# Sample attention over the paged cache: from split 128-column products to plain fp32 products of 32 columns

## The chip, the cores and the metric

The kernel runs on one core of one Trainium2 chip. The metric is the time of one execution on the device in microseconds (us). The engines of a core run side by side: TensorE (PE in the profile: matrix products; its loads of the stationary operand are PEld), VectorE (DVE), ScalarE (ACT), GpSimd (POOL), and SyncE (SP), which issues most of the transfers between DRAM and the on-chip memory SBUF. TensorE writes its products to PSUM. A matrix product holds one operand still (the stationary one: at most 128 rows, the length that is summed, by 128 columns) and streams the other past it (the moving one: up to 512 columns).

## What is computed

One layer of a decoder for 1024 prompt tokens and 64 sample tokens (8 sequences of 8 new tokens): a SwiGLU feed-forward half, a mixing stage (8 heads of forgetting attention and 4 heads of gated linear attention), and a second feed-forward half, all in fp32. The part that matters here is the attention of the sample tokens over a paged cache. Each sequence has 2048 cached positions in 16 pages of 128, found through a page table, for 8 heads of 64:

```python
def fox_sample(q, k, v, logf, pool_k, pool_v, pool_logf, page_table):
    DB, S, H, D = q.shape
    P = page_table.shape[1] * PAGE_SIZE
    pk = pool_k[page_table].reshape(DB, P, H, D)
    pv = pool_v[page_table].reshape(DB, P, H, D)
    ...
    s_past = (jnp.einsum('bqhd,bkhd->bhqk', q, pk).astype(jnp.float32) * scale
              + cn[..., :, None] + jnp.swapaxes(after, 1, 2)[:, :, None, :])
    s_new = (jnp.einsum('bqhd,bkhd->bhqk', q, k).astype(jnp.float32) * scale
             + cn[..., :, None] - cn[..., None, :])
    causal = jnp.tril(jnp.ones((S, S), dtype=bool))
    s_new = jnp.where(causal, s_new, -jnp.inf)
    p = jax.nn.softmax(jnp.concatenate([s_past, s_new], axis=-1), axis=-1).astype(v.dtype)
    return (jnp.einsum('bhqk,bkhd->bqhd', p[..., :P], pv)
            + jnp.einsum('bhqk,bkhd->bqhd', p[..., P:], v))
```

`after` is the sum of the log-forgets of the cached positions behind a key; `cn` the running sum over the new tokens.

## The kernel before

Products of full precision are built from a reduced form of fp32 (float32r), which TensorE takes in one pass: an operand is split into a rounded part `hi` and the rest `lo` (line 143: ScalarE copies with rounding, VectorE subtracts), and a product is the sum of hi·hi, hi·lo and lo·hi. A product of plain fp32 operands is given to TensorE as it is, and the trace records it as two passes, each with its own weight load (line 1228 has 224 such products of 64 columns in its full tiles and 448 records).

The dense products of the feed-forward halves and projections (line 210, line 440) make up most of the work. The program emits them in a fixed order, and `tick` (line 155) hands out other work between them: after so many microseconds of dense products it lets the attention emit a piece. For the sample attention the rate is 1.1 pieces a microsecond (line 985). So it lies spread between dense products, from about 1305 to 1680 us of the span. The order on each engine's queue is that in which the program is laid out, where readiness lets a later product go before an earlier one.

`sample` (line 759) handles two sequences (a pair, `p`) at a time, in steps:

- `fetch` (line 781) loads two pages (128 x 2 x 512 numbers, 512 KB) into a buffer `pr`, five of which exist, three steps ahead of use. Key pages come by SP's queue (`page`, line 749) with the page number read into a register; value pages, and every second key page of the first pair, by an indirect transfer that GpSimd issues (line 791). Every fourth page brings with it the biases `af` (16 rows: hi and lo for 8 heads).
- `cut` (line 798) splits the buffer into `ph` and `pl`, one step ahead, two buffers each.
- `key_step` (line 841): the stationary operand is `qz`, 128 columns: 64 for the hi part of a sequence's queries and 64 for the lo part, with the heads laid out so that pair `a` of heads has 16 columns of each half and zeros elsewhere. For each of four pairs of heads there are two products (lines 854 and 855, with `ph` and `pl`) of 256 moving columns; a ninth product (line 856) adds the biases through `sel`, 16 rows by 128 columns. Each second step, `total` (line 830) adds the halves and keeps the greatest score.
- `new_keys` (line 861): the scores of the new tokens, eight products of 64 columns and one of 16 rows, twice a pair. `soft` (line 870): exponential and scaling of all 2112 scores of 128 rows. `queries` (line 819) places the next pair's queries in the two `qz` tiles, the same two for every pair.
- `turn` (line 877): transposes of the weights, split into `pT`.
- `value_step` (line 894): for each of two pages two products (lines 902 and 903) of 512 moving columns, stationary the 64 hi and 64 lo columns of all heads of one sequence; all heads meet all heads, and only the matching blocks are used. After the eighth step, two products for the new tokens' values (line 906, 64 rows), and the sum goes to `ob`. `out` (line 910) adds the halves and takes the matching blocks, by four products with `fold` (line 914).

For a pair there are 16 key steps, 5 turns and 16 value steps; the next pair's key steps alternate with the value steps.

Of the kernel before, what the change touches and what calls it, by code (L numbers as in the profile page):

```python
# [55 lines left out]
def together(*gens):  # L56
    """Pieces of several streams in turn"""
    live = list(gens)
    while live:
        for g in list(live):  # L60
            if next(g, live) is live:
                live.remove(g)
            else:
                yield


class Feed:
    """Weights in the order of their use: loaded two ahead, split one ahead"""
# [49 lines left out]
class Step:  # L118
# [24 lines left out]
    def split(self, hi, lo, src):  # L143
        """src = hi + lo, hi rounded"""
        self.nc.scalar.copy(hi, src)  # L145
        self.nc.vector.tensor_tensor(out=lo, in0=src, in1=hi.bitcast(F32), op=ALU.subtract)  # L146
# [28 lines left out]
    def beside(self, g, quick=False, begin=False):  # L175
        """Adds a stream of norm or evacuation pieces; begin: its first piece now"""
# [20 lines left out]
    def gemm(self, w, c0, n, packed=False):  # L197
        """Full-precision product of split operands. packed: hi has lo's columns behind its own 64, the sum of the halves is left to do."""
# [15 lines left out]
    def square(self, yk, k, n, pool, sums):  # L214
        """Adds a row of squares to one of two partial sums."""
# [12 lines left out]
    def ptile(self, kind):  # L228
        """A bank of PSUM for the norms: col, col2 or rows"""
# [3 lines left out]
    def rms(self, sums, n, pool, kind):  # L233
        """1/rms of every token, windows of tokens on the partitions"""
# [7 lines left out]
    def rms_quick(self, y, n, pool):  # L242
        """1/rms of the first n tokens, by as many engines as can help"""
# [20 lines left out]
    def rms_col(self, col, m, pool):  # L264
        """1/rms from m pairs of columns of sums"""
# [7 lines left out]
    def stat(self, sums, n, pool, out):  # L273
        """Piece that finishes the sums of a chunk"""
# [9 lines left out]
    def rms_rows(self, dg, n):  # L284
        """[P, n] with 1/rms of every token on all partitions"""
# [5 lines left out]
    def need(self, key):  # L291
        """Emits what is left of the norms up to key"""
# [3 lines left out]
    def norm(self, y, y0, c0, n, pool, post=None, pre=None, v=None, key=None):  # L296
        """post: y = res + rmsnorm(y) * gain, also to DRAM; pre: U = split(rmsnorm(y) * gain). v: list that takes 1/rms. Yields between pieces."""
# [57 lines left out]
    def ffn(self, w_gu, w_dn, f):  # L355
        """Jobs for y = (silu(U wg) * (U wu)) wd, transposed, for the columns of f. f.first(i): before chunk i is used first;
        f.after(c0, n, sums): what follows a finished chunk of y."""
# [9 lines left out]
        def gated(t, src, x):  # L367
            """t = silu(src), or twice that where f.tanh; x: src on the partitions of t"""
# [175 lines left out]
NRAW = 5  # L544
NAF = 3
NHL = 2
AHEAD = 3
# [7 lines left out]
class StepA(Step):  # L555
# [169 lines left out]
    def past_bias(self, pool):  # L725
        """Sum of the log-forgets after every cached position, split, to DRAM."""
# [22 lines left out]
    def page(self, g, dst, pool):  # L749
        """Loads page g of the table from the pool."""  # L750
# [8 lines left out]
    def sample(self, X, ps):  # L759
        """Paged forgetting attention of the sample group, two sequences at a time; yields between pieces."""  # L760
# [3 lines left out]
        tmp = lambda nm, shape, dt: X.tile(shape, dt, name=nm, tag="ob", bufs=1)  # L764
# [7 lines left out]
        qsmp = cst("qsmp", [P, 2, 4, TS], F32R)  # L772
        ksmp = cst("ksmp", [P, 2, 4, TS], F32R)
        vsmp = cst("vsmp", [TS, 2, 512], F32R)
        for s in range(2):
            nc.sync.dma_start(qsmp[:, s].bitcast(F32), self.qs[s, :, :, TP:].rearrange("a p t -> p a t"))
        self.page_dmas = []
        pages = []
        raws, parts, afs = {}, {}, {}

        def fetch(n):
# [4 lines left out]
            for i in range(2):  # L786
                g = 2 * p * NPG + 2 * t + i
# [5 lines left out]
            if kind == "K" and t % 2 == 0:  # L793
                afs[p, t // 2] = af = X.tile([16, 512], F32R, name=self.uid("af"), tag="af", bufs=NAF)
                o = t % 8 // 2 * 512
                nc.sync.dma_start(af.bitcast(F32), self.afs[2 * p + t // 8].rearrange("s h g t -> (s h) (g t)")[:, o:o + 512])

        def cut(n):
            if n in parts or n >= len(pages):
                return  # L800
            hi = X.tile([P, 2, 512], F32R, name=self.uid("ph"), tag="hi", bufs=NHL)
            lo = X.tile([P, 2, 512], F32R, name=self.uid("pl"), tag="lo", bufs=NHL)
            self.split(hi, lo, raws[n])
            parts[n] = hi, lo
# [8 lines left out]
        qz = []  # L813
        for i in range(2):
            z = cst(f"qz{i}", [P, 4, P], F32R)
            nc.scalar.copy(z, self.zero[:, :1].unsqueeze(2).to_broadcast([P, 4, P]))
            qz.append(z)

        def queries(p):
            for b in (2 * p, 2 * p + 1):  # L820
                for s in range(2):
                    for e in range(2):
                        r = slice(64 * e, 64 * e + 64)
                        o = qz[b % 2][r].rearrange("p a n -> p (a n)")
                        o = bass.AP(tensor=o.tensor, offset=o.offset + 64 * s + 8 * e, ap=[o.ap[0], [P + 16, 4], [1, 8]])
                        (nc.gpsimd if p else nc.vector).tensor_copy(o, qsmp[r, s, :, 8 * b:8 * b + 8].bitcast(F32))
# [3 lines left out]
        def total(p, e2, sp, n, o, add, w):  # L830
            """Sum of the two parts of scores, with the greatest"""
            R = slice(64 * e2, 64 * e2 + 64)
            sl = X.tile([64, 512], F32, name=self.uid("sl"), tag="sl", bufs=1)
            if add is None:
                nc.scalar.copy(sl[:, :n], sp[64:, :n])
            else:
                nc.vector.tensor_tensor(out=sl[:, :n], in0=sp[64:, :n], in1=add, op=ALU.add)
            nc.vector.tensor_tensor_reduce(out=S[p][R, o:o + n], in0=sp[:64, :n], in1=sl[:, :n], scale=1.0, scalar=-3.0e38,
                                           op0=ALU.add, op1=ALU.max, accum_out=mx[p][R, w:w + 1])

        def key_step(n, p, t):
            kh, kl = page_step(n)
            q = qz[t // 8]
# [3 lines left out]
            j = t % 2  # L847
            if j == 0:
                box["sp"] = ps.tile([P, 512], F32, name=self.uid("sp"), tag="S", bufs=2)
            sp = box["sp"]  # L850
            cs = slice(256 * j, 256 * j + 256)
            so = sp[:, cs].rearrange("p (g t) -> p g t", t=P)
            for a in range(4):
                nc.tensor.matmul(so, q[:, a, :], kh[:, :, a * P:(a + 1) * P], start=(a == 0), stop=False)  # L854
                nc.tensor.matmul(so, q[:, a, :], kl[:, :, a * P:(a + 1) * P], start=False, stop=False)  # L855
            nc.tensor.matmul(sp[:, cs], sel, afs[p, t // 2][:, cs], start=False, stop=True)  # L856
            if j:
                g = t % 8 // 2
                total(p, t // 8, sp, 512, 512 * g, None, g)

        def new_keys(p):
            for e2 in range(2):
                sp = ps.tile([P, 512], F32, name=self.uid("sp"), tag="S", bufs=2)
                for a in range(4):
                    for s in range(2):
                        nc.tensor.matmul(sp[:, :TS], qz[e2][:, a, :], ksmp[:, s, a, :], start=(a == 0 and s == 0), stop=False)
                nc.tensor.matmul(sp[:, :TS], sel, cnr, start=False, stop=True)
                total(p, e2, sp, TS, NK, smask[:, 2 * p + e2, :], 4)

        def soft(p):  # L870
# [4 lines left out]
            nc.scalar.activation(out=s, in_=s, func=AF.Copy, scale=m[:, 7:8])  # L875

        def turn(p, j):
            if j == 0:
                box["pT"] = X.tile([P, NPG, 2, P], F32R, name=self.uid("pT"), tag="pT", bufs=1)
                box["pN"] = X.tile([64, 2, P], F32R, name=self.uid("pN"), tag="pN", bufs=1)  # L880
            pT, pN, s = box["pT"], box["pN"], S[p]
            tp = ps.tile([P, 512], F32, name=self.uid("tp"), tag="pt", bufs=1)
            if j < 4:
                for i in range(4):
                    nc.tensor.transpose(tp[:, P * i:P * i + P], s[:, (4 * j + i) * P:(4 * j + i + 1) * P], self.ident)
                src = tp.rearrange("p (g e c) -> p g e c", e=2, c=64)
                h, l = pT[:, 4 * j:4 * j + 4, :, :64], pT[:, 4 * j:4 * j + 4, :, 64:]
            else:
                nc.tensor.transpose(tp[:64, :P], s[:, NK:], self.ident)
                src = tp[:64, :P].rearrange("p (e c) -> p e c", c=64)  # L890
                h, l = pN[:, :, :64], pN[:, :, 64:]
            self.split(h, l, src)
# [768 lines left out]
```

## Time and profile before

| | |
|---|---|
| median of 3 runs | 2524.99 us |
| lowest and highest | 2522.19 and 2528.23 us |
| span of the profiled execution | 2529.9 us |
| mean clock granted to TensorE in it | 0.984 of full |
| HBM read, written | 284.39 MB, 43.69 MB |

The span is that of another execution than the three timed ones, from its first instruction to its last; it has no other time of its own. In the profile a line such as "L854 PE MATMUL sp<-ph,qz 128*128 128x256 f32 x256 | 67.9, 291 | 2.4 <-ACT ph L145 2.4" means: line 854 of the kernel, TensorE, products into `sp` from `ph` and `qz`, stationary 128 rows by 128 columns, moving 128 rows by 256 columns, 256 of them; 67.9 us busy together, 291 ns each in the mean; TensorE idle for 2.4 us just before them, all of it until ScalarE had done `ph` on line 145. A line of the timeline gives the start (us from the span's start), the time to the end of the group, and the group. A line of the windows view gives the stretch, its length, the busy time and number of instructions of PE, PEld, DVE, ACT and POOL, the granted clock, the mean busy share of the 16 DMA engines and GB/s. In the view of one line's instructions, three durations are least, median and greatest in ns, then the first and last start. In the view of waits: who waited for whom, us in total, times, longest. Products on TensorE overlap their neighbours, so that what one costs is read from the distance between starts rather than from its own duration.

### The profile page before, as it was taken

What the parts mean: (1) busy time and instruction counts of PE and PEld (TensorE: products, weight loads), DVE (VectorE), ACT (ScalarE), POOL (GpSimd) and SP (SyncE); (2) the same over time, 40 slices, a digit from 0 to 9 for tenths busy, and PEclk for the clock granted to TensorE, in tenths of its full rate; (3) what the DMA queues carried; (4) which work ended last, traced back from release to release, by engine and by line L of the source; (5) the groups of instructions that cost most, each with busy time, mean ns of one, the idle gap of its engine ahead of it and who ended that gap; (6) DMA issues with size and microseconds to landing.
All of it is one profiled execution on the core that took longest, in us unless ns stands there. A gap on an engine that the chain in (4) does not pass through costs nothing.

```text
span 2529.9 us, 40161 instructions
## 1 busy us (share of the span) xinstructions
PE 2469.8 (98%) x15524; PEld 2221.8 (88%) x15524; DVE 1343.8 (53%) x2500; ACT 1021.2 (40%) x1752; POOL 404.8 (16%) x426
## 2 busy tenths in 40 slices
PE   7999999999999999999999999999999999999997
PEld 7799999999899788999897787878788989999997
DVE  7223232322358746655567777757776675333345
ACT  5311112111134556553547666646455544222222
POOL 3000000000013210100233644540010131000001
PEclk9999999999999999999999999999899999999998
DMA  3111111111134776643457776765554544222222
GB/s 121 65 42 44 49 42 43 50 42 43 68 123 131 229 225 190 186 148 102 154 183 239 249 252 223 225 188 155 148 167 136 191 129 149 83 82 83 84 76 88
DMA packets 177024, 330.71 MB, mean 131 GB/s; under 512 B 25265, under 2 KB 100482, under 8 KB 176834
## 3 DMA queue, kind: packets, MB, share of 16 engines
q1 hardware_dynamic: 165170, 289.87, 36.2%
q0 software_dynamic: 11664, 38.28, 4.8%
q8 instruction: 122, 2.00, 0.3%
q14 instruction: 68, 0.56, 0.1%
HBM read 284.39 MB, written 43.69 MB: 130 GB/s over the span
## 4 chain that ended last, share of the span: by engine, by line
PE 39%; issue 4%; DMA 3%; DVE 3%; POOL 2%; ACT 2%; POOLq 0%; ACTq 0%; DVEq 0%; SPq 0%
PE mm L210 17%; PE mm L440 10%; PE pa L1228 1%; DMA pr<-in_cv,rows 1%; PE sp L854 1%; DMA wr<-in_wout 1%; POOL pr L791 1%; PE sp L855 1%; PE tp L1084 1%; DVE wl L146 1%; PE po L1099 1%; PE po L903 1%; PE po L902 1%; ACT wh L145 1%; PE sp L856 1%
## 5 line engine op out<-in xcount | busy, mean ns | idle before, releaser
L210 PE MATMUL mm<-ub,wh 128*128 128x320 f32 (+2 forms) x3776 | 771.5, 299 | 0.1
L210 PE MATMUL mm<-ua,wh 128*128 128x512 f32 (+2 forms) x2288 | 639.1, 364 | 3.8 <-ACT ua L351 1.7
L210 PEld LDWEIGHTS mm<-ub,wh 128*128 128x128 f32 (+1 forms) x3776 | 608.3, 189 | 9.9 <-issue 3.1
L146 DVE TENSOR_TENSOR wl<-wr,wh 128x1024 fp32r<-128x1024 f32 (+1 forms) x294 | 356.8, 1214 | 407.6 <-ACT wh L145 404.7
L145 ACT CAST wh<-wr 128x1024 fp32r<-128x1024 f32 (+1 forms) x294 | 301.4, 1025 | 647.5 <-PE mm L210 305.0
L210 PE MATMUL mm<-ub,wl 128*128 128x320 f32 (+1 forms) x1872 | 553.2, 296 | 0.3 <-DVE wl L146 0.3
L210 PEld LDWEIGHTS mm<-ua,wh 128*128 128x128 f32 (+1 forms) x2288 | 400.8, 191 | 64.9 <-issue 4.9
L210 PE MATMUL mm<-ua,wl 128*128 128x512 f32 (+1 forms) x1136 | 408.4, 360 | 0.8 <-DVE wl L146 0.7
L210 PEld LDWEIGHTS mm<-ub,wl 128*128 128x128 f32 x1872 | 354.4, 189 | 0.5 <-DVE wl L146 0.5
L440 PE MATMUL mm<-hl,wh 128*128 128x256 f32 (+4 forms) x1088 | 354.1, 326 | 0.0
L440 PE MATMUL mm<-hh,wh 128*128 128x256 f32 (+2 forms) x1040 | 339.9, 327 | 0.8 <-DVE y L450 0.8
L440 PE MATMUL mm<-hh,wl 128*128 128x256 f32 (+2 forms) x1040 | 333.0, 321 | 0.0
L210 PEld LDWEIGHTS mm<-ua,wl 128*128 128x128 f32 x1136 | 217.0, 191 | 33.2 <-DVE wl L146 1.8
L450 DVE TENSOR_TENSOR y<-y,mm 128x256 f32<-128x256 f32 (+2 forms) x272 | 130.0, 503 | 185.6 <-PE mm L440 184.9
L224 POOL TENSOR_TENSOR ss<-ss,sq 128x256 f32<-128x256 f32 (+1 forms) x46 | 44.0, 959 | 1146.6 <-ACT sq L220 1145.1
L440 PEld LDWEIGHTS mm<-hl,wh 128*128 128x128 f32 (+1 forms) x1088 | 206.1, 189 | 19.6 <-issue 8.6
L440 PEld LDWEIGHTS mm<-hh,wh 128*128 128x128 f32 x1040 | 196.7, 189 | 18.7 <-issue 4.2
L440 PEld LDWEIGHTS mm<-hh,wl 128*128 128x128 f32 x1040 | 196.9, 189 | 12.3 <-issue 0.6
L146 DVE TENSOR_TENSOR pl<-pr,ph 128x1024 fp32r<-128x1024 f32 x128 | 155.9, 1224 | 69.9 <-ACT ph L145 68.9
L791 POOL DMA_INDIRECT pr<-in_cv,rows x128 | 164.2, 1283 | 117.5 <-DVE pl L146 64.3
L145 ACT CAST ph<-pr 128x1024 fp32r<-128x1024 f32 x128 | 133.6, 1048 | 98.8 <-PE sp L854 45.7
L379 DVE TENSOR_TENSOR sg<-mm,sg 128x256 f32<-128x256 f32 (+4 forms) x112 | 55.8, 498 | 185.9 <-PE mm L210 184.3
(244 smaller groups left out, 2799.8 us busy)
## 6 DMA issues: line engine op xcount, KB each, us to landing
wr<-in_wgu SPq DMA_DIRECT2D x137, 512.0 KB
wr<-in_wd SPq DMA_DIRECT2D x60, 512.0 KB
pr<-in_ck SPq DMA_DIRECT2D x112, 256.0 KB
wr<-in_win SPq DMA_DIRECT2D x50, 512.0 KB
wr<-in_wout SPq DMA_DIRECT2D x32, 512.0 KB
h<-y SPq DMA_DIRECT2D x12, 512.0 KB
x<-h SPq DMA_DIRECT2D x24, 256.0 KB
wr<-in_wd SPq DMA_DIRECT2D x20, 256.0 KB
```

The source lines that it names most:

```text
L145: self.nc.scalar.copy(hi, src)
L146: self.nc.vector.tensor_tensor(out=lo, in0=src, in1=hi.bitcast(F32), op=ALU.subtract)
L210: nc.tensor.matmul(out, a, x[:, k, o:o + n], start=(k == 0 and j == 0), stop=(k == KB - 1 and j == len(ops) - 1))
L224: (nc.gpsimd if odd else nc.vector).tensor_tensor(out=s, in0=s, in1=sq[:, :n], op=ALU.add)
L379: nc.vector.tensor_tensor(out=out, in0=u, in1=t, op=ALU.mult)
L440: nc.tensor.matmul(pds[e], a, b, start=(i == 0 and j == 0), stop=(i == len(g) - 1 and j == len(ops) - 1))
L450: nc.vector.tensor_tensor(out=yk, in0=yk, in1=pds[e], op=ALU.add)
L791: nc.gpsimd.indirect_dma_start(out=raw[:, i], out_offset=None, in_=A["ck" if kind == "K" else "cv"].rearrange("g p n -> (g p) n"), in_offs ...
L854: nc.tensor.matmul(so, q[:, a, :], kh[:, :, a * P:(a + 1) * P], start=(a == 0), stop=False)
L855: nc.tensor.matmul(so, q[:, a, :], kl[:, :, a * P:(a + 1) * P], start=False, stop=False)
L856: nc.tensor.matmul(sp[:, cs], sel, afs[p, t // 2][:, cs], start=False, stop=True)
L902: nc.tensor.matmul(po, pT[:, g, e2, :], vh[:, i], start=(g == 0), stop=False)
```

## The change

The sample attention takes plain fp32 operands: pages are used as they land, without `cut`. The queries and new keys and values, which lie in DRAM as two parts, are loaded and added up once. A stationary operand has 32 columns, those of one pair of heads for both sequences of the pair (2 sequences x 2 heads x 8 queries), and its output goes to one of four groups of 32 PSUM partitions: pair of heads `a` at 32a. A key step's buffer holds two pages of one sequence, with zeros in the other sequence's 16 columns; a value step's holds one page of each sequence. The bias product comes first, once for 512 columns, with `sel` and the biases padded with zeros to 128 rows. There are eight page buffers instead of five, loaded six steps ahead instead of three; each pair of sequences has its own of two `qz` tiles; the softmax's scaling moves to the copy of the output. One accumulation and one `out` serve both sequences. The constants `sel` and `smask` follow the new layout, and `fold` goes. The diff also drops the docstrings, which is left out here.

```diff
-NRAW = 5
+NRAW = 8
 NAF = 3
-NHL = 2
-AHEAD = 3
+AHEAD = 6
...
+        q2 = X.tile([P, 2, 4, TS], F32, name="q2", tag="two", bufs=2)
...
+        nc.vector.tensor_tensor(out=qf, in0=q2[:, 0], in1=q2[:, 1], op=ALU.add)
...
+        afz = [cst(f"afz{i}", [P, 512], F32R) for i in range(NAF)]
+        qz = [cst(f"qz{i}", [P, 4, 2, 32]) for i in range(2)]
+        for z in qz:
+            nc.gpsimd.memset(z, 0.0)
...
-                g = 2 * p * NPG + 2 * t + i
+                if kind == "K":
+                    g = (2 * p + t % 2) * NPG + 4 * (t // 4) + 2 * (t % 4 // 2) + i
+                else:
+                    g = (2 * p + i) * NPG + t
...
-            for m in range(n, n + NHL):
-                cut(m)
-            return parts[n]
+            return raws[n]
...
+        def total(p, sp, n, o, add, w):
+            nc.vector.tensor_tensor_reduce(out=S[p][:, o:o + n], in0=sp[:, :n], in1=add, scale=1.0, scalar=-3.0e38,
+                                           op0=ALU.add, op1=ALU.max, accum_out=mx[p][:, w:w + 1])
...
         def key_step(n, p, t):
-            kh, kl = page_step(n)
-            q = qz[t // 8]
+            raw = page_step(n)
+            j, hf, s = t // 4, t % 4 // 2, t % 2
...
+            if t % 4 == 0:
                 box["sp"] = ps.tile([P, 512], F32, name=self.uid("sp"), tag="S", bufs=2)
+                nc.tensor.matmul(box["sp"], sel, afs[p, j], start=True, stop=False)
             sp = box["sp"]
             for a in range(4):
-                nc.tensor.matmul(so, q[:, a, :], kh[:, :, a * P:(a + 1) * P], start=(a == 0), stop=False)
-                nc.tensor.matmul(so, q[:, a, :], kl[:, :, a * P:(a + 1) * P], start=False, stop=False)
-            nc.tensor.matmul(sp[:, cs], sel, afs[p, t // 2][:, cs], start=False, stop=True)
+                nc.tensor.matmul(sp[32 * a:32 * a + 32, 256 * hf:256 * hf + 256], qz[p % 2][:, a, s, :], raw[:, :, a * P:(a + 1) * P], start=False, stop=(t % 4 == 3))
+            if t % 4 == 3:
+                total(p, sp, 512, 512 * j, self.zero[:, :1].to_broadcast([P, 512]), j)
...
         def new_keys(p):
+            sp = ps.tile([P, 512], F32, name=self.uid("sp"), tag="S", bufs=2)
+            nc.tensor.matmul(sp[:, :TS], sel, cnr, start=True, stop=False)
+            for s in range(2):
                 for a in range(4):
+                    nc.tensor.matmul(sp[32 * a:32 * a + 32, :TS], qz[p % 2][:, a, s, :], kf[:, a, :], start=False, stop=(s == 1))
+            total(p, sp, TS, NK, smask[:, p, :], 4)
...
-            nc.scalar.activation(out=s, in_=s, func=AF.Copy, scale=m[:, 7:8])
...
+                nc.scalar.copy(pT[:, 4 * j:4 * j + 4, :].rearrange("p g c -> p (g c)"), tp)
...
         def value_step(n, p, t):
-            vh, vl = page_step(n)
+            raw = page_step(n)
...
-                nc.tensor.matmul(po, pT[:, g, e2, :], vh[:, i], start=(g == 0), stop=False)
-                nc.tensor.matmul(po, pT[:, g, e2, :], vl[:, i], start=False, stop=False)
...
+            for a in range(4):
+                r = slice(32 * a, 32 * a + 32)
+                nc.tensor.matmul(po[r], pT[:, t, r], raw[:, :, a * P:(a + 1) * P], start=(t == 0), stop=False)
+            if t == NPG - 1:
+                for a in range(4):
+                    r = slice(32 * a, 32 * a + 32)
+                    nc.tensor.matmul(po[r], pN[:, r], vf[:, :, a * P:(a + 1) * P], start=False, stop=True)
+                box["ob"] = X.tile([P, 2 * P], F32, name=self.uid("ob"), tag="ob", bufs=2)
+                nc.scalar.activation(out=box["ob"], in_=po, func=AF.Copy, scale=mx[p][:, 7:8])
...
-                nc.tensor.matmul(ot[:, 64 * a:64 * a + 64], ob[:, a * P:(a + 1) * P], fold, start=True, stop=True)
+            for s in range(2):
+                nc.tensor.transpose(ot[:, s * P:(s + 1) * P], ob[:, s * P:(s + 1) * P], self.ident)
```

More of the change, by code (lines that the diff above doesn't have):

```diff
@@ L792, in fetch @@
                                                  in_offset=bass.IndirectOffsetOnAxis(ap=rows[:, g:g + 1], axis=0))
[L793 to L804, printed above, removed]
+            if kind == "K" and t % 4 == 0:
+                j = t // 4
+                afs[p, j] = af = afz[(4 * p + j) % NAF]
+                for s in range(2):
+                    nc.sync.dma_start(af[16 * s:16 * s + 16].bitcast(F32), self.afs[2 * p + s].rearrange("s h g t -> (s h) (g t)")[:, 512 * j:512 * j + 512])
         def page_step(n):
@@ L904, in value_step @@
-            if j == 7:
-                for s in range(2):
-                    nc.tensor.matmul(po, box["pN"][:, e2, :], vsmp[:, s, :], start=False, stop=(s == 1))
-                box["ob"] = X.tile([P, 512], F32, name=self.uid("ob"), tag="ob", bufs=1)
-                nc.scalar.copy(box["ob"], po)
-        def out(b):
+            po, pT = box["po"][:, :2 * P], box["pT"]
+            for a in range(4):
+                r = slice(32 * a, 32 * a + 32)
+                nc.tensor.matmul(po[r], pT[:, t, r], raw[:, :, a * P:(a + 1) * P], start=(t == 0), stop=False)
@@ L945, in sample @@
                     paged("K", p + 1, ks.pop(0))
-            outs = {}
-            for t in range(16):
+            for t in range(NPG):
                 paged("V", p, t)
-                if t % 8 == 7:
-                    outs[t // 8] = len(steps)
-                if t == 9 or t == 15:
-                    if t == 15 and not ks:
-                        steps.append(lambda: None)
-                    steps.append(lambda b=2 * p + t // 10: out(b))
                 if ks:
@@ L958, in sample @@
                         scored(p + 1)
+            steps.append(lambda: None)
+            steps.append(lambda p=p: out(p))
+        for z in afz:
+            nc.scalar.copy(z, self.zero[:, :1].to_broadcast([P, 512]))
         for n in range(AHEAD):
@@ L961, in sample @@
         queries(0)
+        k2 = X.tile([P, 2, 4, TS], F32, name="k2", tag="two", bufs=2)
         for s in range(2):
-            nc.sync.dma_start(ksmp[:, s].bitcast(F32), self.ks[s, :, :, TP:].rearrange("a p t -> p a t"))
-            nc.sync.dma_start(vsmp[:, s].rearrange("t (a v) -> t a v", v=P).bitcast(F32), self.vss[:, s].rearrange("a t v -> t a v"))
-        fold = cst("fold", [P, 64])
-        smask = cst("smask", [64, NB, TS])
-        nc.sync.dma_start(fold, A["fold"])
+            nc.sync.dma_start(k2[:, s], self.ks[s, :, :, TP:].rearrange("a p t -> p a t"))
+        kf = cst("kf", [P, 4, TS])
+        nc.vector.tensor_tensor(out=kf, in0=k2[:, 0], in1=k2[:, 1], op=ALU.add)
+        v2 = X.tile([TS, 2, 512], F32, name="v2", tag="v2", bufs=1)
+        for s in range(2):
+            nc.sync.dma_start(v2[:, s].rearrange("t (a v) -> t a v", v=P), self.vss[:, s].rearrange("a t v -> t a v"))
+        vf = cst("vf", [P, 2, 512])
+        nc.gpsimd.memset(vf, 0.0)
+        for i in range(2):
+            nc.vector.tensor_tensor(out=vf[:TS, i], in0=v2[:, 0], in1=v2[:, 1], op=ALU.add)
+        pN = cst("pN", [P, P])
+        nc.gpsimd.memset(pN, 0.0)
+        smask = cst("smask", [P, NB // 2, TS])
         nc.sync.dma_start(smask, A["smask"])
-        selr = tmp("selr", [16, P], F32)
+        selr = tmp("selr", [P, P], F32)
         nc.sync.dma_start(selr, A["sel"])
-        sel = cst("sel", [16, P], F32R)
+        sel = cst("sel", [P, P], F32R)
         nc.scalar.copy(sel, selr)
-        cnr = cst("cnr", [16, TS], F32R)
-        nc.sync.dma_start(cnr.bitcast(F32), self.cns.rearrange("s h t -> (s h) t"))
+        cnr = cst("cnr", [P, TS], F32R)
+        nc.scalar.copy(cnr, self.zero[:, :1].to_broadcast([P, TS]))
+        for s in range(2):
+            nc.sync.dma_start(cnr[16 * s:16 * s + 16].bitcast(F32), self.cns.rearrange("s h t -> (s h) t"))
         for _ in range(LEAD):
@@ L1597, in consts @@
     c['later']=((i[:,None]//16==i[None]//16)&(i[:,None]%16>i[None]%16)).astype(np.float32)
[L1598 to L1600 removed]
+    t=np.arange(64); s_,q_=i[:,None,None]//16%2,i[:,None,None]%8; p_=np.arange(4)[None,:,None]
+    c['smask']=np.where((t//8==2*p_+s_)&(t%8<=q_),0,-1e30).astype(np.float32)
     r=np.ones((128,512+64),np.float32); r[:,0:512:128]=0; r[:,512::8]=0; c['rst']=r
[L1602 to L1604 removed]
+    s=np.zeros((128,128),np.float32)
+    for a in range(32):
+        h=a%8
+        o=32*(h//2)+16*(a//16)+8*(h%2)
+        s[a,o:o+8]=1
     c['sel']=s
```

82 lines of the change are left out of this document (19 added, 63 removed).

## The prediction

> **What bounds the kernel now.** I read the page's busy table first, then the windows view for the stretch in which the sample attention runs (its pages are loaded from 1305 us on, its last product starts at 1679 us), then that stretch by line and shape.
>
> ```profile
> PE 2469.8 (98%) x15524; PEld 2221.8 (88%) x15524; DVE 1343.8 (53%) x2500; ACT 1021.2 (40%) x1752; POOL 404.8 (16%) x426
> ...
> 1300.00:1680.00 380.00, 368.85 (x1875) 296.99 (x1876) 270.80 (x373) 234.48 (x289) 198.00 (x174) 0.98 0.71 228
> ```
>
> TensorE is busy 98% of the span, and in this stretch 368.85 of 380 us; VectorE 271, ScalarE 234, the DMA share 0.71. So TensorE's own time counts one for one, and work taken off ScalarE and VectorE counts only through TensorE's 11 idle us. By line and shape:
>
> ```profile
> L146 DVE TENSOR_TENSOR pl<-pr,ph 128x1024 fp32r<-128x1024 f32 x128 | 155.9, 1224 | 69.9 <-ACT ph L145 68.9
> L145 ACT CAST ph<-pr 128x1024 fp32r<-128x1024 f32 x128 | 133.6, 1048 | 98.8 <-PE sp L854 45.7 <-PE po L902 24.6 <-DMA pr<-in_cv,rows 18.4
> L854 PE MATMUL sp<-ph,qz 128*128 128x256 f32 x256 | 67.9, 291 | 2.4 <-ACT ph L145 2.4
> L855 PE MATMUL sp<-pl,qz 128*128 128x256 f32 x256 | 64.4, 284 | 0.9 <-DVE pl L146 0.9
> L902 PE MATMUL po<-ph,pT 128*128 128x512 f32 x128 | 52.6, 411 | 6.8 <-ACT ob L908 5.0 <-ACT ph L145 1.7
> L903 PE MATMUL po<-pl,pT 128*128 128x512 f32 x128 | 52.4, 410 | 1.1 <-DVE pl L146 0.9
> L856 PE MATMUL sp<-af,sel 16*128 16x256 f32 x64 | 24.0, 377 | 0.0
> ```
>
> The splits of the pages (289 us of two engines) go away whole, but TensorE waited only 2.4 + 0.9 + 6.8 + 1.1 = 11.2 us in front of these products. The question is what the products themselves cost. A row's mean overlaps its neighbours, so I price by the distance between starts in the timeline of TensorE:
>
> ```profile
> 1403.84 0.28 PE L855 MATMUL sp<-pl,qz 128*128 128x256 f32 x1
> 1403.95 0.28 PE L854 MATMUL sp<-ph,qz 128*128 128x256 f32 x1
> 1404.08 0.28 PE L855 MATMUL sp<-pl,qz 128*128 128x256 f32 x1
> 1404.28 0.38 PE L856 MATMUL sp<-af,sel 16*128 16x256 f32 x1
> 1404.59 0.50 PE L902 MATMUL po<-ph,pT 128*128 128x512 f32 x1
> 1404.93 0.62 PE L210 MATMUL mm<-ua,wh 128*128 128x512 f32 x2
> 1405.39 0.39 PE L903 MATMUL po<-pl,pT 128*128 128x512 f32 x1
> 1405.62 0.40 PE L902 MATMUL po<-ph,pT 128*128 128x512 f32 x1
> ```
>
> A 256-column product takes 0.12 us, a 512-column one 0.23. The 16-row bias product costs more than itself: 0.20 to it instead of 0.12, 0.31 over it, 0.34 over the next instead of 0.23: 0.08 + 0.31 + 0.11 = **0.50 us**, of which 0.11 is its own stream. So an excursion from the full array to a tile of it and back costs **0.39 us**.
>
> **The change part by part.** *Price of a plain fp32 product.* Line 1297 (one such product, 512 columns) is recorded as two passes:
>
> ```profile
> 1923.87 1.02 PE L1297 MATMUL rb<-gsq,ones 128*128 128x512 f32 x2
> 1924.33 1.02 PE L210 MATMUL mm<-ua,wh 128*128 128x512 f32 x2
> 1925.18 0.40 PE L210 MATMUL mm<-ua,wl 128*128 128x512 f32 x1
> ```
>
> From 1923.87 to 1925.18 are 1.31 us; two dense products take 0.46 of it, so two passes of 512 columns take 0.85, and one pass of 256 columns 0.21. Each page step of the new kernel has four products of two passes: 8 x 0.21.
>
> *What four column positions make of it.* No row shows two tiles of the array at work, so I bound it. One after another: 8 x 0.2135 = 1.71 us. All four side by side: 2 x 0.2135 = 0.43. I take the middle that the timeline's strict order suggests: its rows start one by one as the program has them. The second pass of a position needs the columns that the first one occupies, and waits; the next position's first pass stands behind it and can run beside it. So one pass-time goes by per position, and one at the end: 5 x 0.2135 = **1.07 us**.
>
> *Excursions.* Every page step now leaves the full array. 0.39 us is for weights of 128 columns; a load of few columns is shorter:
>
> ```profile
> L706 PEld LDWEIGHTS lt<-ident,st x9: 80/85/88, 875.4 to 1059.0; 128*8 128x8 f32 x8, 64*8 64x8 f32 x1
> L856 PEld LDWEIGHTS sp<-af,sel x64: 180/181/185, 1324.3 to 1613.9; 16*128 16x128 f32 x64
> ```
>
> 0.085 against 0.181 for 8 and 128 columns, so 32 columns save 0.08 once: **0.31 us**. The bounds are 0 (column positions might need no change-over) and 0.39. Here a page speaks against the change: the Trainium skill, TensorEngine Tiling (Array Packing), section Key Properties, says that changing the tiling mode drains the engine, while changing the tile does not. The row tiles above agree (0.39 us); no run yet shows column tiles; by the page the 128 excursions stay in the sum, without it they leave it.
>
> *Sum of TensorE's sample work, before.* Besides the page steps:
>
> ```profile
> 1364.48 0.97 PE L866 MATMUL sp<-ksmp,qz 128*128 128x64 f32 x8
> 1365.39 0.29 PE L867 MATMUL sp<-cnr,sel 16*128 16x64 f32 x1
> 1365.61 0.73 PE L210 MATMUL mm<-ua,wh 128*128 128x512 f32 x2
> 1366.17 0.28 PE L854 MATMUL sp<-ph,qz 128*128 128x256 f32 x1
> ...
> 1676.73 0.40 PE L903 MATMUL po<-pl,pT 128*128 128x512 f32 x1
> 1677.06 0.73 PE L906 MATMUL po<-vsmp,pN 64*128 64x512 f32 x2
> 1677.72 0.50 PE L210 MATMUL mm<-ua,wh 128*128 128x512 f32 x1
> 1678.06 0.40 PE L210 MATMUL mm<-ua,wl 128*128 128x512 f32 x1
> ...
> 1678.98 1.00 PE L914 MATMUL ot<-fold,ob 128*128 128x64 f32 x8
> 1679.79 0.71 PE L210 MATMUL mm<-ua,wh 128*128 128x512 f32 x2
> 1680.34 0.39 PE L210 MATMUL mm<-ua,wl 128*128 128x512 f32 x1
> ```
>
> Each group is the distance to its follower plus what the follower is late. Keys 64 x 8 x 0.1175 = 60.2; bias 64 x 0.50 = 32.0; values 256 x 0.23 = 58.9; new keys 8 x 1.23 = 9.8 (1.13 + 0.10); new values 8 x 0.87 = 7.0 (0.10 + 0.66 + 0.11); fold 8 x 0.90 = 7.2. Together **175.1 us**.
>
> *After.* Keys 64 x (1.07 + 0.31) = 88.3; values the same 88.3; bias 16 full-array products of 512 columns, 16 x 0.23 = 3.7; new keys 4 x (0.12 + 0.31 + about 0.6 for 16 short passes) = 4.1; new values, behind the last value step, 4 x 0.85 = 3.4; output 8 transposes x 0.11 (the fold's 0.90 / 8) = 0.9. Together **188.7 us: 13.6 more**.
>
> *Stalls.* Of the 11.2 idle us, the 5.0 for `ob` go (one accumulation for two sequences, with five turns before the next), and those for the splits too, but the first page's landing stays. I take **10 off** (bounds 0 and 11). Late next is a page's landing: 4.5 us in the median, now asked for six steps ahead into eight buffers, with a step about 2.5 us apart; that hides it. On GpSimd the wait that held the value pages' loads behind it goes, since the query tiles now alternate between pairs:
>
> ```profile
> POOL qz L826 <- PE sp L866: 19.8, 3, 15.8
> POOL pr L791 <- DVE pl L146: 84.3, 36, 8.4
> ```
>
> Its second wait becomes one for TensorE's step three earlier, long done. SP's queue carries as many page loads as before, and the weight loads behind them wait less, for the same reason. The new clears and sums of halves (about ten operations of 0.2 to 2 us) lie on ScalarE, VectorE and GpSimd ahead of the first step, beside dense products; uncovered, they would cost some 3 us. The softmax loses its scaling of 2112 columns, ScalarE work that TensorE hides.
>
> *The sum.* 13.6 - 10 = +3.6 us on the profiled span of 2529.9, that is 2533.5. The median of the runs shown, 2525.0, is 4.9 below that span (the span is one execution, slightly above the slowest of them, 2528.2); less 4.9 the forecast is **2528.5 us**, +0.1%. Its own range: excursions at nothing take 40 off (2489), at 0.39 with the stalls left 20 on (2549).
>
> **The rivals.** *Real side-by-side.* If both passes of all four positions overlap, a step is 0.43 + 0.02 + 0.31 = 0.76 us: 97.3 for the page steps, 3.7 + 2.5 + 1.7 + 0.9 for the rest, 106.1 in all: 69 less, with the stalls 79, so **2446**. For it: the streams read and write different columns. Against: the strict order of starts. It can't be had whole if transfers run short: 0.71 x 380 / 301 would be a DMA share of 0.90, and the most of any 40 us here is 0.81:
>
> ```profile
> 1580.00:1620.00 40.00, 40.00 (x206) 32.56 (x205) 30.55 (x43) 22.91 (x27) 25.95 (x23) 1.00 0.81 256
> ```
>
> At 0.81 the stretch is 333 us, 47 less: 2478. So 2406 (no excursion cost) to 2478. The Trainium skill, TensorE: Matmul & The Clock Gate, Part 3, says that matmuls on different column tiles start some 4 ns apart and gives a 2.38-fold gain for three; that is this rival. The same section calls starts and ends strictly ordered, which with two passes a product is my forecast; no row here decides it.
>
> *No side-by-side (slower).* The positions do not do what they are for: each pass waits for the one before. Steps cost 1.71 + 0.31 = 2.02: 258.6 + 3.7 + 5.2 + 6.8 + 0.9 = 275.2, 100 more; less the stalls' 10, **2615** (2575 without excursions, 2635 with all of them). For it: no row shows two tiles overlapping. It decides from (175.1 + 10 - 12.1) / 128 = 1.35 us a step on, excursion included: above that the kernel is slower, and the forecast's 1.38 lies close to it.
>
> **How the numbers follow.** Forecast 0.56, side by side 0.26, one after another 0.18. About 0.2% (5 us) is what a measurement of this kernel can tell from no change. Within the forecast, 2489 to 2549 around that band: 0.17 faster, 0.18 the same, 0.21 slower. With the rivals: faster 0.43, same 0.18, slower 0.39. Both signs hold most of the chance, so the likeliest case's own range, 2489 to 2549, stands beside the whole one: 2440 to 2590, which leaves out most of the slow rival and the tail of the fast one.
>
> **What would show it.** In the timeline, the starts of a step's eight passes: steps of 0.21 in pairs (a second pass beside the next position's first) bear out the forecast; all within 0.25 us the fast rival; 1.5 us from first to last the slow one. The distance from the last pass to the next dense product, and from the dense one before, gives the excursion. Page casts gone from ScalarE and VectorE, and under 2 us of idle time before the products, bear out the stalls; a new wait of TensorE for `pr` would prove them wrong, as would a DMA share of 0.85 and more in the stretch.

## The result, and the profile after

| | before | after |
|---|---|---|
| median of 4 runs | 2524.2 us | **2444.14 us** |
| lowest and highest | 2522.19 and 2528.23 us | 2440.27 and 2454.03 us |
| ratio of after to before, 95% interval | | 0.9687 (0.9659 to 0.9715) |
| span of the profiled execution | 2529.9 us | 2452.3 us |

The change makes the kernel 80 us faster. The forecast was 2528.5, almost no change; the time lies inside the range, 2 us from the rival "real side-by-side" (2446).

The busy table of the page, after:

```profile
PE 2392.2 (98%) x15688; PEld 2105.6 (86%) x15688; DVE 1170.8 (48%) x2300; ACT 863.0 (35%) x1582; POOL 359.2 (15%) x418
```

TensorE still is what bounds the kernel: busy for 98% of a shorter span. VectorE lost 173 us and ScalarE 158, yet that is not where the time came from, as the runs with the splits put back show below. The windows view of the sample stretch of each kernel shows where it did (stretch, length, busy time and instructions of PE, PEld, DVE, ACT and POOL, granted clock, DMA share, GB/s). The first fence is before, the second after:

```profile
1305.00:1680.00 375.00, 363.90 (x1836) 292.05 (x1835) 265.80 (x363) 231.76 (x283) 196.27 (x171) 0.98 0.72 230
```

```profile
1314.00:1604.00 290.00, 281.95 (x2004) 171.21 (x2003) 91.55 (x163) 74.55 (x112) 150.75 (x165) 0.98 0.86 296
```

The stretch is 85 us shorter, and the span 77.6. TensorE's busy time alone fell by 82 us in it. The dense products in the two stretches are nearly the same (line 440 has 232 in each, line 210 451 of 512 columns and 101 of 256 before, 434 and 122 after). So the products of the sample attention themselves became cheaper, where the forecast had them 13.6 us dearer. By line and shape, after, from 1290 to 1620 us:

```profile
L837 PE MATMUL sp<-pr,qz 128*32 128x256 f32 x512 | 51.2, 399 | 1.9 <-DMA pr<-in_ck 1.9
L875 PE MATMUL po<-pr,pT 128*32 128x256 f32 x512 | 50.9, 388 | 2.1 <-DMA pr<-in_cv,rows 2.1
L834 PE MATMUL sp<-afz,sel 128*128 128x512 f32 x16 | 6.8, 422 | 0.9 <-ACT sel L951 0.9
```

512 records are 64 steps of eight passes. The mean of one is 0.39 us, as long as that of a 512-column dense product, and says nothing of its price, since it overlaps its neighbours. The price stands in the timeline of TensorE, here around one value step (start, time to the end of the group, group):

```profile
1581.05 0.40 PE L210 MATMUL mm<-ua,wl 128*128 128x512 f32 x1
1581.38 0.64 PE L875 MATMUL po<-pr,pT 128*32 128x256 f32 x8
1581.95 0.72 PE L210 MATMUL mm<-ua,wh 128*128 128x512 f32 x2
1582.51 0.40 PE L210 MATMUL mm<-ua,wl 128*128 128x512 f32 x1
```

From 1581.05 to the step are 0.33 us (0.23 between dense products), from the step to the next dense product 0.57, and that product's follower is 0.10 late (0.56 for two products that take 0.46). A step costs 0.10 + 0.57 + 0.10 = **0.77 us**. Eight passes one after another would take 1.71 us by themselves. Where two steps stand together, the narrow windows of the timeline show passes starting in fours, at 1450.59, 1450.83, 1451.05 and 1451.26, one pass-time apart:

```profile
1450.59 0.42 PE L837 MATMUL sp<-pr,qz 128*32 128x256 f32 x4
...
1450.83 0.40 PE L837 MATMUL sp<-pr,qz 128*32 128x256 f32 x4
...
1451.05 0.40 PE L875 MATMUL po<-pr,pT 128*32 128x256 f32 x4
...
1451.26 0.40 PE L875 MATMUL po<-pr,pT 128*32 128x256 f32 x4
```

That bears out four positions that take their first pass together and then their second, though the records don't name positions. A step is 2 x 0.2135 = 0.43 us, and the change-over 0.77 - 0.43 = **0.34 us**.

### The profile page after: what moved, and what is told of

The parts are those of the page before. It is cut to its first block, busy times and chain, and to the rows that moved or that the text cites. A ratio compares the mean times of both kernels' runs of the same rounds, so it can differ in the third digit from the quotient of the medians.

```text
span 2452.3 us, 39759 instructions
## 1 busy us (share of the span) xinstructions
PE 2392.2 (98%) x15688; PEld 2105.6 (86%) x15688; DVE 1170.8 (48%) x2300; ACT 863.0 (35%) x1582; POOL 359.2 (15%) x418
## 4 chain that ended last, share of the span: by engine, by line
PE 38%; issue 4%; DVE 3%; DMA 2%; POOL 2%; ACT 1%; SPq 0%; POOLq 0%; ACTq 0%; DVEq 0%
PE mm L210 20%; PE mm L440 10%; PE sp L837 1%; PE po L875 1%; DMA wr<-in_wout 1%; PE pa L1209 1%; PE tp L1065 1%; PE po L1080 1%; DVE wl L146 1%; POOL pr L798 1%; ACT wh L145 1%; POOL y L328 0%; PE s L1047 0%; DMA pr<-in_cv,rows 0%; PE s L1048 0%
## 5 line engine op out<-in xcount | busy, mean ns | idle before, releaser
L440 PEld LDWEIGHTS mm<-hh,wh 128*128 128x128 f32 x1040 | 196.5, 189 | 23.2 <-issue 11.1
L798 POOL DMA_INDIRECT pr<-in_cv,rows x128 | 128.3, 1003 | 98.1 <-PE po L875 41.2
L145 ACT CAST hh<-sg 128x320 fp32r<-128x320 f32 (+2 forms) x128 | 62.6, 489 | 213.1 <-DVE sg L379 170.0
L373 ACT ACTIVATE sg<-mm 128x256 f32<-128x256 f32 (+4 forms) x112 | 49.1, 439 | 143.8 <-PE mm L210 143.6
```

Of the source, the lines that this page charges most:

```text
L373: nc.scalar.activation(out=t, in_=src, func=AF.Silu)
L440: nc.tensor.matmul(pds[e], a, b, start=(i == 0 and j == 0), stop=(i == len(g) - 1 and j == len(ops) - 1))
L798: nc.gpsimd.indirect_dma_start(out=raw[:, i], out_offset=None, in_=A["ck" if kind == "K" else "cv"].rearrange("g p n -> (g p) n"), in_offs ...
```

## The experiments

Two theories stood after the result. **A**: the four column positions work at the same time, each at its own pace, and that is the gain. **B**: the positions give little, the order of starts stays strict, and the time comes from elsewhere (splits gone, deeper loading, fewer products).

### All steps at one position

```diff
+                b = (0, 0, 0, 0)[a] if t % 4 < 3 else a
-                nc.tensor.matmul(sp[32 * a:32 * a + 32, ...
+                nc.tensor.matmul(sp[32 * b:32 * b + 32, ...
...
+                b = (0, 0, 0, 0)[a] if t else a
-                nc.tensor.matmul(po[r], ...
+                nc.tensor.matmul(po[32 * b:32 * b + 32], ...
```

The same products, operands and loads. In 108 of the 128 steps (48 of 64 with keys, 60 of 64 with values) all four pairs of heads are summed into position 0, so scores and outputs mix the heads.

> The changed kernel, but in 48 of the 64 key steps and 60 of the 64 value steps all four products go to the first column position (their sum is then not the attention's; number, shapes and loads stay). Theory A, the gain is the overlap of positions: eight passes of 0.2135 us one after another, 1.71 instead of 0.43 us a step, so 108 x 1.28 = 138 us more than the changed kernel, about 2582 us. Rival B, the gain came from dropping the splits and the shorter loads of weights, not from the positions: within 10 us of 2444.

Measured in a single run: 2580.47 us (before, beside it, 2521.98). That is 136 us above the changed kernel. The timeline around one value step:

```profile
1501.78 0.40 PE L440 MATMUL mm<-hh,wl 128*128 128x512 f32 x1
1502.11 1.91 PE L877 MATMUL po<-pr,pT 128*32 128x256 f32 x8
1503.95 0.50 PE L440 MATMUL mm<-hh,wh 128*128 128x512 f32 x1
1504.29 0.39 PE L440 MATMUL mm<-hl,wh 128*128 128x512 f32 x1
```

From the step to the next dense product are 1.84 us, against 0.57 with four positions. The difference, 1.27, is six pass-times of 0.2135 (1.28); times 108 steps it is 138 us. So overlap of positions is worth the whole gain and more: at one position, with the splits gone and the deeper loading kept, the kernel is 58 us slower than before. This is the mechanism of the prediction's slow rival, which put 2615 us on all 128 steps.

### Two positions, in two orders

The same edit with `(0, 0, 1, 1)`, and with `(0, 1, 0, 1)`. If products have to start as the program has them, the first order is the worse by far, since the second product of position 0 holds up those of position 1. If each position goes on by itself, the order doesn't matter.

> As the kernel with one position, but with two positions in the program order 0, 0, 1, 1. Theory A, a pass starts as soon as its own position is free, whatever stands before it for another position: four pass-times a step, 0.85 instead of 0.43, 108 x 0.43 = 46 us more than the changed kernel, about 2490. Rival B, starts in strict program order (the prediction's step): 0, 0 takes four pass-times before the first pass of position 1 starts, beside the last of position 0; seven pass-times, 1.49 us, 108 x 1.07 = 115 us more, about 2559.

> The same two positions in the order 0, 1, 0, 1. Theory A (each position goes on by itself): four pass-times as in the order 0, 0, 1, 1, the same time within 5 us, about 2490. Rival B (strict program order): five pass-times, 1.07 us, 108 x 0.64 = 69 us more than the changed kernel, about 2513, and 46 us less than the order 0, 0, 1, 1.

Measured in a single run each: 2479.63 for 0, 0, 1, 1 and 2490.67 for 0, 1, 0, 1. The strict order's figure for the first is 79 us too high, and the order that it calls worse is not the slower one. In the first kernel's timeline, a key step; the last line is from the narrow window 1507.70 to 1507.90:

```profile
1507.44 0.39 PE L834 MATMUL sp<-afz,sel 128*128 128x512 f32 x1
1507.75 1.06 PE L838 MATMUL sp<-pr,qz 128*32 128x256 f32 x8
1508.75 0.72 PE L210 MATMUL mm<-ua,wh 128*128 128x512 f32 x2
...
1507.75 0.42 PE L838 MATMUL sp<-pr,qz 128*32 128x256 f32 x2
```

Two passes start together. At one position passes come one after another, as the kernel before this one showed, so one of the two is position 1's. 1.00 us from the step to the next dense product is 0.43 more than 0.57, two pass-times: four passes at each of two positions, side by side, though the program has all four of position 0 first. That settles the step of the prediction that failed. The 11 us between the two kernels don't come from the order. The views of line 838, first for 0, 0, 1, 1 and then for 0, 1, 0, 1:

```profile
L838 PE MATMUL sp<-pr,qz x512: 376/379/404, 1319.2 to 1573.1; 128*32 128x256 f32 x171
L838 PE MATMUL sp<-pr,qz x512: 375/379/404, 1331.1 to 1581.3; 128*32 128x256 f32 x171
```

The second kernel reaches its first key product 11.9 us later, before any product in which the two differ; the granted clock from 1000 us up to there was 0.98 in the first and 0.95 in the second. From that product to the start of the last value product (line 877) are 307.2 us in the first and 303.3 in the second: in the sample stretch itself the two orders lie within 4 us.

### The splits put back

Every page again gets ScalarE's rounding copy and VectorE's subtraction; nothing reads the result.

```diff
+        cuts = set()
...
         def page_step(n):
             for m in range(n, n + AHEAD):
                 fetch(m)
+            for m in range(n, min(n + 2, len(pages))):
+                if m not in cuts:
+                    cuts.add(m)
+                    hi = X.tile([P, 2, 512], F32R, name=self.uid("ph"), tag="hi", bufs=2)
+                    lo = X.tile([P, 2, 512], F32R, name=self.uid("pl"), tag="lo", bufs=1)
+                    self.split(hi, lo, raws[m])
```

Beside it on the same chip ran the changed kernel itself.

> The changed kernel again, as the measure for the other runs on this chip: 2444 us, ratio 0.969.

> The changed kernel with the split of every page put back on ScalarE and VectorE (133 and 156 us of work), into tiles that nothing reads; TensorE's work stays. Theory A, TensorE bounds the stretch and the splits' time was hidden: within 5 us of the changed kernel. Rival B, part of the gain is the relief of ScalarE and VectorE: slower by 10 us or more.

Measured: the changed kernel 2442.89 (ratio 0.9645, 0.9618 to 0.9672), with the splits 2468.86 (0.974, 0.9708 to 0.9771). The expectation that ScalarE and VectorE hide them failed by 26 us. The product on the value pages waits for its page (by line, from the whole span):

```profile
L882 PE MATMUL po<-pr,pT 128*32 128x256 f32 x512 | 53.1, 398 | 8.7 <-DMA pr<-in_cv,rows 8.7
```

A split holds its page's buffer, so the next page is ordered later. That could be the reason, or the load on the two engines. To part them, the splits were made of a fixed tile of zeros, which holds no page (`self.split(..., fixed...)` instead of `raws[m]`). It ran on another chip, and beside it again the changed kernel:

> The changed kernel again, as the measure for the three beside it: 2443 us (2436 to 2452), 0.9645 to 0.969 of the kernel before.

> Every page step again gives ScalarE one copy and VectorE one subtraction of a page's size, but of a fixed tile of zeros, so that no page buffer is held by them; nothing reads their results. Theory A, the load on the two engines delays what TensorE waits for: about +26 us over the changed kernel as in the run that split the pages themselves, some 2469 us. Theory B, that run lost its time because a page's buffer came free only after its split, so that the next page was ordered later: within 6 us of the changed kernel, 2437 to 2449 us. Between the two, both count, in the share that the time shows.

Measured: the changed kernel 2462.87 here (0.9731, 0.9704 to 0.9759), 20 us more than on the chip before, while the kernel before the change took 2529.51 on this and 2532.51 on the other. With the fixed splits 2463.82: no difference. Since the yardstick itself had moved, all three were run once more on a third chip:

> The changed kernel, as the measure for the two beside it on the same chip: 2443 us if TensorE idles under 10 us in the 290 us of the sample stretch, 2463 if it idles some 16 us with 6 of them for nothing that the profile shows, as in the two earlier runs of it.

> The splits of every page put back on the two engines, results unread. Theory A, it is the late release of the page buffers: 20 to 30 us over the changed kernel beside it, whatever that one's time. Theory B, the 26 us of the first such run were of its chip: within 8 us of the changed kernel beside it.

> The same load on the two engines from a fixed tile, so that no page buffer is held. Theory A, only held buffers cost: within 8 us of the changed kernel beside it. Theory C, the load itself costs: 20 us or more over it, like the run beside it.

Measured: changed kernel 2466.69 (0.9713 to 0.9824), splits of the pages 2470.46 (0.9739 to 0.9838), splits of a fixed tile 2455.79 (0.965 to 0.9735). The last two intervals both overlap with the changed kernel's. So the load on the two engines costs nothing that these runs show, as predicted, on both chips on which it ran. Splits that hold the page buffers took 2469 and 2470 us on both of their chips; they cost 26 us where the changed kernel runs at 2443 and nothing that shows where it runs at 2467. What makes that difference between chips is not settled. The windows view of the changed kernel, 1300 to 1610 us, on the chip where it took 2442.89 and then where it took 2462.87:

```profile
1300.00:1610.00 310.00, 301.11 (x2119) 188.21 (x2119) 106.24 (x191) 83.08 (x130) 156.34 (x171) 0.98 0.86 291
```

```profile
1300.00:1610.00 310.00, 293.77 (x2016) 177.99 (x2014) 96.22 (x175) 76.43 (x117) 153.08 (x167) 0.96 0.84 281
```

TensorE idles 8.9 us on the one and 16.2 on the other, at a clock of 0.98 and 0.96, and the transfers run a little slower. In the view of TensorE's waits on the second chip, part of the idle time is put down to nothing that the profile shows ("issue"):

```profile
PE po L879 <- issue: 3.6, 3, 1.5
PE ot L887 <- DMA pr<-in_ck: 3.0, 1, 3.0
PE mm L440 <- DVE wt L487: 1.8, 1, 1.8
PE mm L440 <- issue: 1.4, 3, 0.5
```

In the first chip's rows of that stretch no such wait appears. From the first key product (line 837) to the last value product (line 879) are 263.6 us on the first chip and 280.2 on the second, so the difference arises in this stretch. The 7 us more of idle time and 2% of clock (about 6 us of 310) are most of these 17; why they arise on some chips was not tried. In all four measurements of the changed kernel (2442.89 to 2466.69) it was faster than the kernel before, by 2.3 to 3.6%.

### The loading depth of the kernel before

```diff
-NRAW = 8
+NRAW = 5
-AHEAD = 6
+AHEAD = 3
```

> The changed kernel with five page buffers and pages asked for three steps ahead, as before. A step now passes in about 2.2 us, so three steps are 6.6 us against a landing of 5.6 us in the median. Theory A, pages come late now and then: 5 to 20 us more than the changed kernel, as TensorE's idle time before the page products. Rival B, the depth is not needed: within 3 us.

Measured beside the 2442.89: 2479.61 (0.9776, 0.9749 to 0.9803), 37 us more, well above what was expected. By line and shape, 1300 to 1640 us:

```profile
L875 PE MATMUL po<-pr,pT 128*32 128x256 f32 x512 | 57.8, 402 | 29.9 <-DMA pr<-in_cv,rows 29.6
L837 PE MATMUL sp<-pr,qz 128*32 128x256 f32 x512 | 53.9, 393 | 0.7 <-DMA pr<-in_ck,rows 0.7
```

TensorE waits 29.6 us for value pages. A wait can cost more than its length. In the changed kernel's own profile the longest wait for a page is followed by a lower granted clock (timeline, then windows view):

```profile
1599.44 0.64 PE L875 MATMUL po<-pr,pT 128*32 128x256 f32 x8 [2.08 <-DMA pr<-in_cv,rows]
```

```profile
1600.00:1603.40 3.40, 3.40 (x20) 2.30 (x13) 0.00 (x0) 0.89 (x2) 0.00 (x0) 0.56 0.00 0
```

The clock was 1.00 from 1596 to 1599 us and 0.56 for these 3.4, so that about 1.5 us are lost on top of the wait's 2.08. With the old products, three pages ahead were enough; with short steps they are not. In the profile before, TensorE stood 11.2 us in front of these products in all, so no more than that could hang on the depth there; 37 of the 80 us hang on it now.

### Fewer change-overs

In the built program the 132 groups of tile products (128 page steps, 4 for new keys) stand in only 100 places between full-array products, because a key step and a value step often come together. Two steps to a piece at half the rate (`RATES = 0.55`, a `yield` after each second step) bring 84 places; four at a quarter of the rate 69; four with 10 buffers and 8 pages ahead 61.

> The changed kernel with two steps at a time between the dense products, at half the rate, so that page products of two steps stand side by side. In the changed kernel's program the 132 groups of page and new-key products stand in 100 places between full-array products. Theory A, each place costs 0.34 us of change-over: some 34 places less, about 12 us less than the changed kernel. Rival B, change-over between column positions and full array costs nothing and the 0.34 us is latency paid by each step: within 3 us.

> Four page steps a piece, with a quarter of the rate: in the program the 560 tile products then stand in 69 places between full-array products, not in 100. Theory A, each change-over of 0.34 us is on the path: 31 x 0.34 = 10.5 us faster than the changed kernel, about 2432 us. Theory B, the pages are what comes last, and TensorE waits longer before a cluster of steps for what it saves between them: 2443 us within 5, with over 10 us of idle time before the page products where the changed kernel has 4.9.

> The same with 10 page buffers and 8 pages ordered ahead instead of 8 and 6; 61 places. Theory A, change-overs and the last stalls both go: 39 x 0.34 = 13 us and 3 of the 4.9 us of idle time, about 2427 us. Theory B, the transfers set the pace of the stretch (their share is 0.87 already): 2440 us or more, with a DMA share of 0.9 in the stretch.

Measured: two steps 2446.06 (0.9643, 0.9616 to 0.9671) beside 2442.89; four steps 2463.58 (0.9738, 0.9714 to 0.9762) and four with deeper loading 2467.46 (0.9748, 0.9724 to 0.9773), both beside 2462.87. None gains. With two steps only 16 places go (16 x 0.34 = 5 us, near what the runs can tell), fewer than the expectation had counted on. For four steps 10.5 us should have shown. What took them is in the waits: summed over the rows by line from 1300 to 1610 us, TensorE idles 24.0 us with four steps and 23.9 with the deeper ones, against 16.1 in the changed kernel on that chip. The 8 us more are mostly "issue" (13.3 and 13.5 us against 6.2), so theory B's shift into waits is seen, but not for the pages as it had said; nor do the transfers set the pace with the deeper loading, for their share is 0.81 from 1300 to 1610 us, not 0.9. Two of the rows with four steps, by line from 1320 to 1610 us:

```profile
L875 PE MATMUL po<-pr,pT 128*32 128x256 f32 x512 | 47.8, 395 | 3.9 <-issue 3.3
L440 PE MATMUL mm<-hh,wl 128*128 128x512 f32 x68 | 27.8, 410 | 1.8 <-issue 1.7
```

What TensorE waits for there stays open, and no run shows the 0.34 us of a change-over saved on the whole time. That it is paid once for a place, and not by each step, is read from the changed kernel's timeline, around a key step and a value step that stand together:

```profile
1450.26 0.40 PE L834 MATMUL sp<-afz,sel 128*128 128x512 f32 x1
1450.59 0.64 PE L837 MATMUL sp<-pr,qz 128*32 128x256 f32 x8
1451.05 0.61 PE L875 MATMUL po<-pr,pT 128*32 128x256 f32 x8
1451.59 0.50 PE L440 MATMUL mm<-hh,wh 128*128 128x512 f32 x1
1451.92 0.39 PE L440 MATMUL mm<-hl,wh 128*128 128x512 f32 x1
```

The two steps take 1.00 us and 0.10 on either side, 1.20 in all: four pass-times (0.85) and one change-over, 0.35. No version here beats the changed kernel beyond what the runs can tell.

## Why the prediction was wrong

- **What bounds the kernel** was right: TensorE's time counts one for one, and the 82 us that it lost in the stretch are the gain.
- **The price of a pass** was right: 0.2135 us forecast, 0.21 to 0.24 between the starts of fours.
- **"One pass-time goes by per position, and one at the end: 5 x 0.2135 = 1.07 us"** is the step that failed. It took the strict order of starts, seen in rows of products that all use the same columns, for a rule on products that don't. Measured: 0.43, the bound "all four side by side". Over 128 steps the error is 128 x 0.64 = 82 us, nearly the whole of the miss of 84. A position does wait for its own second pass, as the prediction said, but the next position doesn't stand behind it.
- **The change-over** was forecast at 0.31 and is 0.34 by the timeline. It is paid 100 times, not 132, since steps of two kinds stand together; this the prediction could have counted. The Trainium skill, TensorEngine Tiling (Array Packing), Key Properties, says that a change of the tiling mode drains the engine. The 0.34 us bear out that the change costs time; that it is a drain no view shows.
- **The sum** with these sizes: 128 x 0.43 + 100 x 0.34 + 7.6 for the rest (the fast rival's 8.8 less the new keys' four change-overs, which are among the 100) = 96.6 us against 175.1, so -78.5.
- **The stalls**: -10 forecast. Idle time before these products went from 11.2 to 4.9 us, so -6.3; the pages' own landing took the place of the splits. So the term was 4 us too large. Both signs that the prediction had set against it came: TensorE waits 4.0 us for `pr`, and the DMA share is 0.86. The loads of value pages on GpSimd also wait for TensorE's value steps, which the prediction had called long done:

```profile
POOL pr L798 <- PE po L875: 41.2, 26, 4.8
```

- **The account of the stretch**: -78.5 and -6.3 are -84.8, and the stretch is 85.0 shorter. That they meet so closely is luck: TensorE's busy time fell by 82.0, not 78.5, and its idle time in the stretch by 3.1 (11.1 to 8.1), since it waits elsewhere too. Some 7 us were lost again outside (the span's gain is 77.6): in the profiled execution the stretch begins 9 us later than before. From 1000 to 1200 us the granted clock was 0.98 before and 0.93 after, which is some 10 us. That need not be the change's: in two other executions of the changed kernel, on the second and third chip, it was 0.97 and 0.99 there.
- **The cover**: that ScalarE and VectorE hide the splits held as far as load goes; the deeper loading, which the prediction named as what hides a page's landing but gave no price, is worth 37 us once the steps are short. The prediction had set it against 2.5 us a step, with its own long steps.
- **The rivals**: the fast one named the right mechanism and came within 2 us. Luck has a part in that: it has 41 us for change-overs (132 at 0.31) where 34 were paid, takes 4 us too much off for the stalls, and has nothing for the 7 us lost outside the stretch. Its doubt, a DMA share of at most 0.81, fell: 0.86 in the stretch. As a sign against the stalls ("a DMA share of 0.85 and more") it was a poor one, since the idle time before these products fell all the same. The slow rival's mechanism doesn't occur, but one position alone does show its price.
- **The range** held, because the fast rival's bounds were in it; the chance of 0.56 stood on an order that no row had shown for tiles.

## What to carry to other kernels

Before pricing products on parts of the array, ask which columns each one occupies: in these runs, products on different column positions with their own PSUM partitions waited for one another only within a position, whatever their order in the program. Each excursion from the full array took about a third of a microsecond in the timeline, so count the places where it happens, not the products; that fewer places make a kernel faster was not shown here. And when steps become short, ask anew how far ahead their operands have to be loaded: what was hidden under long steps becomes the next bound.

## What the runs showed of the hardware

Products of TensorE on different column positions don't start in the order of the program. At 1454 us of the changed kernel's profile the built program has, between two dense products, value product V0 (position 0), key products K0 to K3, and V1 to V3. The timeline:

```profile
1454.31 0.40 PE L875 MATMUL po<-pr,pT 128*32 128x256 f32 x1
1454.32 0.42 PE L837 MATMUL sp<-pr,qz 128*32 128x256 f32 x3
1454.55 0.38 PE L875 MATMUL po<-pr,pT 128*32 128x256 f32 x1
1454.56 0.58 PE L837 MATMUL sp<-pr,qz 128*32 128x256 f32 x4
1454.78 0.39 PE L875 MATMUL po<-pr,pT 128*32 128x256 f32 x3
1454.98 0.38 PE L837 MATMUL sp<-pr,qz 128*32 128x256 f32 x1
1454.99 0.39 PE L875 MATMUL po<-pr,pT 128*32 128x256 f32 x3
1455.32 0.50 PE L440 MATMUL mm<-hh,wl 128*128 128x512 f32 x1
```

The records don't name positions, but the counts do: one value product and three key products start together, V0 at position 0 and K1 to K3 at the free ones. The fourth, K0, can only come behind V0's second pass, when K1 to K3, which follow it in the program, have had both of theirs. Sixteen passes take four pass-times, from 1454.31 to 1455.32 with the change-over. The Trainium skill, TensorE: Matmul & The Clock Gate, Part 3, says that matmuls start and end strictly in the program's order; between column positions this trace differs, and the measurement decides.

With four positions and two passes a product, the gain of a step is 1.71 / 0.43, fourfold, before the change-over. The Trainium skill, TensorE: Matmul & The Clock Gate, Part 3, gives a measured gain of 2.38 for three column tiles; no run here has three.
